# The lo parts of phase 1 on VectorE: weight splits and turned parts leave GpSimd, which keeps the rotation of q and k

## The chip, the cores and the metric

The kernel runs on one core of one Trainium2 chip. The metric is device time in microseconds of one launch, the median of several runs. The program is written in a tile framework that puts the instructions of each engine into a fixed order when the kernel is built, by a timeline that it plays through itself; on the chip every engine works through its own queue in that order and waits on semaphores of the others.

## What is computed

One layer of a decoder over a prompt of 2048 tokens (width 1024) and 8 decode tokens. What matters here is its front part:

```python
h = rmsnorm(x, g_mix) * (1 + sc_m) + sh_m
proj = h @ w_in                                   # 1024 -> 2560
conv_in, q, k, v = split(proj)                    # 1024, 512, 512, 512 columns
u = conv_in[..., :512] * sigmoid(conv_in[..., 512:])
conv_out = silu(layernorm(causal_dwconv(u_ext, dw_w, dw_b)))   # width 31
q, k = partial_rope(q), partial_rope(k)           # first 16 of each 64 columns are rotated
```

Attention with two softmax maps per head, the output projection and a SwiGLU network follow; the change does not touch their code. All of it is float32.

## The kernel before

**Numbers in two parts.** The matrix products are made from operands split in two: `hi` is the float32 value rounded to the matmul type (a copy on ScalarE, ACT), and `lo = raw - hi` is a subtraction. A product is three matmuls (`mm3`, lines 152 to 156): hi by lo, lo by hi, hi by hi. `split_sb` (lines 187 to 189) does both steps for an operand that lies in SBUF; its last argument names the engine of the subtraction, and without one it is GpSimd (POOL).

**Phase 1** (`phase1`, from line 288) makes the projections. It is a row of ten units: k, conv 0, v, conv 1, q for the first 1024 tokens, then conv 0, k, conv 1, v, q for the second (lines 556 to 584). A unit takes 512 columns of `w_in`. `weights` (line 400) loads them as eight raw tiles of 128x512, one for each block of 128 input channels, and splits each (line 414): `wh` on ACT, `wl` on POOL for blocks 0, 2, 4 and 6 (`POOLW`, line 43) and on VectorE (DVE) for the other four. There are 9 buffers for `wh` (line 42), so that one block of the next unit can be split ahead of time and the others when the unit before them lets its own go. `wl` and the raw tiles share 12 slots, and the `wl` of a block is written into the slot of the raw tile one block before it (line 398), so each split waits for the one before.

A **conv unit** (line 450) makes two groups of 128 channels, each as two blocks of 512 tokens: 24 matmuls for the gate, 24 for the value. The product with the sigmoid goes into `u` (line 470, DVE), and the depthwise convolution is a chain of one instruction of 1024 columns on DVE at line 474 and 30 at line 477, each adding one tap to `y`. These chains, 8 of them with 240 instructions at line 477, are most of the work of DVE.

A **nat unit** (line 519; k, v or q) makes eight tiles of 128 tokens by 512 columns: 24 matmuls into `one` (two buffers), then `ev` on ACT (line 531, two buffers), for q and k the rotation in place on POOL (`rope`, lines 498 to 501, four small instructions), a store, and in `emit` (line 503) the split of the turned tile into `parts` (two buffers): hi on ACT, lo on POOL for every v tile and for the even tiles of q and k, on DVE for their odd tiles (lines 511 and 516). `parts` is stored (lines 512, 517) and read back by attention. All loads and stores are issued from one queue (SP), at lines 123 and 126.

Between the tiles of the units, `turn` (line 357) prepares the next 512 tokens: transposes on the tensor engine (PE), `hx` on ACT, `hTh` on ACT and `hTl` on DVE. `ada_steps` (line 428) puts matmuls of 9 rows between the others.

Of the kernel before, what the change touches and what calls it, by code (L numbers as in the profile page):

```python
# [27 lines left out]
HD = 64  # L28
# [11 lines left out]
CONV_LATE = 0  # L40
XB, YB, SGB = 4, 2, 1
WHB, WSL, ASL = 9, 12, 3
POOLW = (0, 2, 4, 6)

# [36 lines left out]
class Kern:  # L83
# [204 lines left out]
    def phase1(self, ctx):  # L288
        nc, tc, I, O = self.nc, self.tc, self.I, self.O
# [8 lines left out]
        if True:  # L298
# [101 lines left out]
            def weights(src, c0, c1=None):  # L400

                out = []
                for k in range(KD):
# [9 lines left out]
                    wh = self.t(wp, [P, 512], F32R, "wh", bufs=WHB)  # L413
                    self.split_sb(wh, wl, raw, nc.gpsimd if k in POOLW else nc.vector)
                    out.append((wh, wl))
# [87 lines left out]
            def emit(kind, dst, tt):  # L503
                rows = slice(tt * P, (tt + 1) * P)
                b, own = tt // 4, slice((tt % 4) * P, (tt % 4 + 1) * P)
                if kind != "q":
                    self.st(O[kind + "_prompt"][0, 0].rearrange("t h d -> t (h d)")[rows], dst)
                pt = self.t(wp, [P, 2 * NH * P], F32R, "parts", bufs=2)
                if kind == "v":
                    v = pt.rearrange("p (i n) -> p i n", i=2)  # L510
                    self.split_sb(v[:, 0], v[:, 1], dst)
                    self.st(self.vD[b][own].rearrange("t i n -> t (i n)"), pt.bitcast(F32))
                else:

                    v = pt.rearrange("p (g r d) -> p g r d", r=2, d=HD)
                    self.split_sb(v[:, :, 0], v[:, :, 1], dst.rearrange("p (g d) -> p g d", d=HD), nc.vector if tt % 2 else None)
                    self.st((self.kD if kind == "k" else self.qD)[b][own].rearrange("t h r d -> t (h r d)"), pt.bitcast(F32))

            def nat_unit(kind, half, then=()):
                w = weights(I["w_in"], {"q": 1024, "k": 1536, "v": 2048}[kind])  # L520
                for i in range(8):
                    if i in then:
                        then[i]()
                    tt = 8 * half + i
                    hh, hl = hT[tt // 4]
                    po = self.ps1()
                    ts_ = slice((tt % 4) * P, (tt % 4 + 1) * P)
                    for k in range(KD):
                        self.mm3(po, hh[:, k, ts_], hl[:, k, ts_], w[k][0], w[k][1], k == 0, k == KD - 1)
                    ev = self.t(wp, [P, 512], F32, "ev", bufs=2)  # L530
                    nc.scalar.activation(ev, po, AF.Copy, scale=QSCALE if kind == "q" else 1.0)  # L531
                    if kind != "v":
                        rope(ev, tab[:, tt, :], P)
                    emit(kind, ev, tt)
                if half == 0:
                    pd = dec_proj(w)
                    ev = self.t(wp, [P, 512], F32, "ev", bufs=2)[:DEC]
                    nc.scalar.activation(ev, pd[:DEC], AF.Copy, scale=QSCALE if kind == "q" else 1.0)
                    if kind != "v":
                        rope(ev, tabd, DEC)  # L540
                    self.st({"q": self.qsD, "k": self.ksD, "v": self.vsD}[kind], ev)
                    if kind != "q":
                        self.st(O[kind + "_sample"].rearrange("o b s h d -> (o b s) (h d)"), ev)
# [994 lines left out]
```

## Time and profile before

| | us |
|---|---|
| median of 3 runs | 2752.56 (2746.84 to 2755.15) |
| the profiled execution | 2752.62 |
| its span, first to last instruction | 2750.4 |

Mean granted TensorE clock 0.974. Busy shares of the span: PE 94%, its weight loads 79%, DVE 70%, ACT 46%, POOL 52%.

A line of the profile names the line of the kernel, the engine, the operation and the tiles that it writes and reads. Idle time of an engine is put down to what released it. Two things need care: matmuls are pipelined, so that a duration of 0.39 us stands beside a start-to-start distance of 0.23 us; and an instruction that waits inside its engine, having been started, counts as busy.

### The profile page before, as it was taken

The page shows a single profiled execution, that of the slowest core. Times are in us where ns is not written, and L with a number is a line of the kernel's source. Part 1 is how long each engine was busy: PE and PEld are TensorE (multiplying, and loading weights), DVE is VectorE, ACT ScalarE, POOL GpSimd, SP SyncE. Part 2 cuts the span into 40 slices and gives each one's busy share as a digit, 9 for nine tenths or more (in the row PEclk, how much of TensorE's full clock was granted, in tenths as well). Part 3 has the DMA queues.
Part 4 walks back from the last instruction along what each step waited for, and adds up shares of the span by engine and source line. Part 5 has one row for each costly group of instructions (what it writes and reads, how often), then busy time and mean ns, then how long its engine had stood idle before and what let it go on. Part 6 is the DMA issues. An engine that isn't in the chain of part 4 may idle for free.

```text
span 2750.4 us, 38187 instructions
## 1 busy us (share of the span) xinstructions
PE 2572.3 (94%) x13470; PEld 2162.1 (79%) x13470; DVE 1921.5 (70%) x2833; ACT 1252.6 (46%) x2385; POOL 1422.3 (52%) x974
## 2 busy tenths in 40 slices
PE   8998999997899997999799999999999999999997
PEld 3475767676688766787799999999899997777875
DVE  2267889995988878767677777676866652455467
ACT  4433231225798766373436343553444334333333
POOL 2125355444732223233576877677877753464573
PEclk9999999998999998999899999999999999999998
DMA  8634232336732223252334333434334435766555
GB/s 277 203 110 175 66 131 100 119 137 185 233 97 89 85 81 124 99 166 100 107 123 144 113 125 113 154 113 127 110 121 131 131 113 195 249 204 223 161 175 181
DMA packets 343993, 391.25 MB, mean 142 GB/s; under 512 B 31829, under 2 KB 258272, under 8 KB 343794
## 3 DMA queue, kind: packets, MB, share of 16 engines
q1 hardware_dynamic: 335945, 370.80, 41.7%
q10 hardware_dynamic: 7856, 18.01, 1.9%
q8 instruction: 106, 1.74, 0.3%
q14 instruction: 86, 0.70, 0.1%
HBM read 283.10 MB, written 106.12 MB: 142 GB/s over the span
## 4 chain that ended last, share of the span: by engine, by line
PE 54%; DVE 9%; issue 7%; POOL 7%; DMA 3%; ACT 2%; SPq 1%; ACTq 0%; POOLq 0%; DVEq 0%
PE in L1161 26%; PE o L1341 10%; PE one L155 2%; PE one L156 2%; PE one L154 2%; DVE p L660 2%; POOL wl L189 1%; PE two L655 1%; PE two L656 1%; PE x L844 1%; PE x L154 1%; POOL w L1273 1%; POOL z L1273 1%; PE x L156 1%; PE x L155 1%
## 5 line engine op out<-in xcount | busy, mean ns | idle before, releaser
L1341 PE MATMUL o<-b,a 128*128 128x512 f32 x1848 | 433.3, 396 | 14.1 <-POOL b L189 11.8
L1341 PEld LDWEIGHTS o<-b,a 128*128 128x128 f32 x1848 | 348.9, 189 | 97.9 <-POOL b L189 12.5
L1161 PE MATMUL in<-cls,wh 128*128 128x344 f32 x1056 | 336.0, 325 | 30.4 <-DVE nat L1164 13.4
L189 POOL TENSOR_TENSOR wl<-wr,wh 128x512 fp32r<-128x512 f32 x198 | 294.2, 1494 | 112.9 <-ACT wh L188 111.8
L1161 PE MATMUL in<-chs,wl 128*128 128x344 f32 x1056 | 341.9, 324 | 7.8 <-DVE wl L189 7.8
L477 DVE SCALAR_TENSOR_TENSOR y<-u,cw,y 128x1024 f32<-128x1024 f32 x240 | 338.5, 1439 | 2.7
L1161 PE MATMUL in<-chs,wh 128*128 128x344 f32 x1056 | 339.9, 322 | 0.0
L1161 PE MATMUL in<-cla,wh 128*128 128x344 f32 x792 | 256.6, 324 | 1.2 <-ACT wh L188 0.7
L188 ACT CAST wh<-tr 128x512 fp32r<-128x512 f32 x264 | 162.3, 618 | 205.0 <-PE in L1161 179.7
L1161 PE MATMUL in<-cha,wl 128*128 128x344 f32 x792 | 254.9, 322 | 0.0
L1161 PE MATMUL in<-cha,wh 128*128 128x344 f32 x792 | 252.4, 321 | 0.0
L189 POOL TENSOR_TENSOR wl<-tr,wh 128x512 fp32r<-128x512 f32 x132 | 203.8, 1548 | 83.4 <-ACT wh L188 79.6
L672 POOL TENSOR_TENSOR p<-p,p 128x384 f32<-128x384 f32 (+9 forms) x60 | 109.1, 1819 | 260.3 <-ACT p L671 210.5
L1161 PEld LDWEIGHTS in<-cls,wh 128*128 128x128 f32 x1056 | 199.4, 190 | 34.0 <-DVE nat L1164 14.0
L1161 PEld LDWEIGHTS in<-chs,wl 128*128 128x128 f32 x1056 | 200.9, 190 | 8.9 <-DVE wl L189 8.9
L189 POOL TENSOR_TENSOR b<-wr,b 128x512 fp32r<-128x512 f32 x77 | 126.0, 1650 | 156.4 <-ACT b L188 155.1
L189 POOL TENSOR_TENSOR w<-w,wh 128x512 fp32r<-128x512 f32 x40 | 86.0, 2150 | 231.6 <-ACT wh L188 113.0
L1161 PEld LDWEIGHTS in<-chs,wh 128*128 128x128 f32 x1056 | 201.4, 191 | 0.0
L189 DVE TENSOR_TENSOR a<-gr,a 128x1032 fp32r<-128x1032 f32 (+1 forms) x77 | 116.4, 1518 | 109.7 <-ACT a L188 109.5
L154 PE MATMUL one<-w,hTh 128*128 128x512 f32 x384 | 156.6, 411 | 16.1 <-ACT ev L531 10.3
L188 ACT CAST wh<-wr 128x512 fp32r<-128x512 f32 x198 | 122.4, 620 | 104.0 <-POOL wl L189 43.9
L664 ACT ACTIVATE p<-p,st 128x384 f32<-128x384 f32 (+15 forms) x128 | 156.1, 1221 | 25.1 <-DVE st L660 20.1
(353 smaller groups left out, 6554.9 us busy)
## 6 DMA issues: line engine op xcount, KB each, us to landing
wr<-in_w_ffn_in SPq DMA_DIRECT2D x132, 512.0 KB
gD<-xt SPq DMA_DIRECT2D x64, 516.0 KB
wr<-in_w_ffn_out SPq DMA_DIRECT2D x99, 256.0 KB
gr<-gD SPq DMA_DIRECT2D x44, 516.0 KB
w<-in_w_in SPq DMA_DIRECT2D x80, 256.0 KB
gr<-gD SPq DMA_DIRECT2D x33, 512.0 KB
xt<-in_x_prompt SPq DMA_DIRECT2D x32, 512.0 KB
a<-in_w_ada SPq DMA_DIRECT2D x64, 256.0 KB
```

The lines of the kernel that those rows point to most:

```text
L154: mm(ps, lhsT=wh, rhs=xl, start=start, stop=False)
L155: mm(ps, lhsT=wl, rhs=xh, start=False, stop=False)
L156: mm(ps, lhsT=wh, rhs=xh, start=False, stop=stop)
L188: self.nc.scalar.copy(out=hi, in_=raw)
L189: (eng or self.nc.gpsimd).tensor_tensor(out=lo, in0=raw, in1=hi.bitcast(F32), op=ALU.subtract)
L477: nc.vector.scalar_tensor_tensor(out=y, in0=u[:, j:j + HALF], scalar=self.cw[:, ct, j:j + 1], in1=y, op0=ALU.mult, op1=ALU.add)
L660: dv.tensor_tensor_reduce(out=pc[:, lo:hi], in0=sc[:, 0:w], in1=add, scale=1.0, scalar=m, op0=ALU.add, op1=ALU.min, accum_out=mo)
L664: nc.scalar.activation(pc[:, 0:L], pc[:, 0:L], AF.Exp, bias=m, scale=-1.0, accum_out=l)
L672: nc.gpsimd.tensor_tensor(out=a, in0=a, in1=b, op=ALU.add)
L1161: nc.tensor.matmul(ps, lhsT=wt[:, k, :], rhs=xt[:, k, :], start=not more and k == 0 and j == 0, stop=k == 3 and j == 2, skip_group_check=True)
L1273: op = lambda e, o, x, y, k: e.tensor_tensor(out=o, in0=x, in1=y, op=k)
L1341: mm = lambda x, y, s, e: nc.tensor.matmul(ps[i], lhsT=a[:, x, sl], rhs=b[:, y], start=s, stop=e, skip_group_check=True)
```

## The change

`POOLW` becomes empty, so that all eight `wl` of a unit are made on DVE, and the `parts` of all tiles of v, q and k get their lo on DVE. The rotation (lines 498 to 501) stays on POOL. That is 10 units by 4, or 40, weight splits and 16 v tiles and 16 even tiles of q and k, or 32, splits of `parts`: 72 instructions of 128x512 change engine. ACT, PE and the transfers get the same instructions as before.

```diff
-POOLW = (0, 2, 4, 6)
+POOLW = ()
...
                 if kind == "v":
                     v = pt.rearrange("p (i n) -> p i n", i=2)
-                    self.split_sb(v[:, 0], v[:, 1], dst)
+                    self.split_sb(v[:, 0], v[:, 1], dst, nc.vector)
...
                     v = pt.rearrange("p (g r d) -> p g r d", r=2, d=HD)
-                    self.split_sb(v[:, :, 0], v[:, :, 1], dst.rearrange("p (g d) -> p g d", d=HD), nc.vector if tt % 2 else None)
+                    self.split_sb(v[:, :, 0], v[:, :, 1], dst.rearrange("p (g d) -> p g d", d=HD), nc.vector)
```

## Rows read from the trace of the kernel before

**Rows 1.** The page: span, and busy time of each engine.

```profile
span 2750.4 us, 38187 instructions
PE 2572.3 (94%) x13470; PEld 2162.1 (79%) x13470; DVE 1921.5 (70%) x2833; ACT 1252.6 (46%) x2385; POOL 1422.3 (52%) x974
```

**Rows 2.** Busy time by stretch: length, PE, PEld, DVE, ACT, POOL, granted clock, DMA.

```profile
138.00:414.00 276.00, 257.08 (x1051) 181.56 (x1050) 213.83 (x201) 82.47 (x128) 122.70 (x76) 0.97 0.35 120
414.00:620.00 206.00, 193.40 (x791) 146.49 (x790) 192.52 (x161) 45.19 (x77) 99.59 (x72) 0.98 0.33 119
```

**Rows 3.** What PE waited for, 138 to 620 us: total, times, longest.

```profile
PE one L154 <- ACT ev L531: 9.3, 1, 9.3
PE two L155 <- POOL w L189: 8.7, 7, 2.1
PE one L154 <- DVE w L189: 4.4, 2, 4.0
PE two L155 <- DVE w L189: 3.1, 6, 1.4
```

**Rows 4.** Groups by line, 138 to 650 us: busy, mean ns, idle before.

```profile
L477 DVE SCALAR_TENSOR_TENSOR y<-u,cw,y 128x1024 f32<-128x1024 f32 x240 | 338.5, 1439 | 2.7
L500 POOL TENSOR_TENSOR rope<-ev,tab 128x64 f32<-128x64 f32 x25 | 22.8, 913 | 0.0
```

**Rows 5.** Line 189, 138 to 650 us: ns min/median/max, first and last start.

```profile
L189 DVE TENSOR_TENSOR w<-w,wh x36: 677/680/1775, 137.3 to 603.9; 128x512 fp32r<-128x512 f32 x36
L189 POOL TENSOR_TENSOR w<-w,wh x35: 1263/2128/13826, 139.0 to 600.3; 128x512 fp32r<-128x512 f32 x35
L189 POOL TENSOR_TENSOR parts<-ev,parts x28: 1262/1504/22977, 205.7 to 641.6; 128x512 fp32r<-128x512 f32 x28
L189 DVE TENSOR_TENSOR parts<-ev,parts x13: 677/693/1750, 142.4 to 647.6; 128x512 fp32r<-128x512 f32 x13
```

**Rows 6.** Timeline, 560 to 563 us, POOL and DVE: start, duration.

```profile
560.03 1.29 POOL L189 TENSOR_TENSOR parts<-ev,parts 128x512 fp32r<-128x512 f32 x1 [2.19 <-ACT parts L188]
...
560.04 2.36 DVE L477 SCALAR_TENSOR_TENSOR y<-u,cw,y 128x1024 f32<-128x1024 f32 x1
...
562.33 1.27 DVE L477 SCALAR_TENSOR_TENSOR y<-u,cw,y 128x1024 f32<-128x1024 f32 x1
```

**Rows 7.** Timeline, 203 to 233 us, POOL, DVE and ACT.

```profile
205.73 24.20 POOL L189 TENSOR_TENSOR parts<-ev,parts 128x512 fp32r<-128x512 f32 x2 [4.01 <-ACT parts L188]
...
217.94 9.64 DVE L477 SCALAR_TENSOR_TENSOR y<-u,cw,y 128x1024 f32<-128x1024 f32 x8
...
228.74 0.60 ACT L531 ACTIVATE ev<-one 128x512 f32<-128x512 f32 x1 [14.46 <-POOL parts L189]
```

**Rows 8.** Timeline, 260 to 278 us, start of a conv unit, DVE.

```profile
267.58 0.69 DVE L189 TENSOR_TENSOR w<-w,wh 128x512 fp32r<-128x512 f32 x1
268.19 1.28 DVE L477 SCALAR_TENSOR_TENSOR y<-u,cw,y 128x1024 f32<-128x1024 f32 x1
...
271.80 0.68 DVE L189 TENSOR_TENSOR w<-w,wh 128x512 fp32r<-128x512 f32 x1
```

**Rows 9.** Timeline, 580 to 592 us, start of the last q unit, DVE and ACT.

```profile
579.79 10.69 DVE L477 SCALAR_TENSOR_TENSOR y<-u,cw,y 128x1024 f32<-128x1024 f32 x8
590.40 0.68 DVE L189 TENSOR_TENSOR w<-w,wh 128x512 fp32r<-128x512 f32 x1
...
582.64 0.62 ACT L188 CAST wh<-w 128x512 fp32r<-128x512 f32 x1
```

**Rows 10.** Busy time by stretch, as rows 2, around two of the waits.

```profile
230.00:240.00 10.00, 10.00 (x39) 8.00 (x38) 2.49 (x3) 5.46 (x8) 2.94 (x3) 0.81 0.83 299
...
590.00:600.00 10.00, 7.53 (x20) 5.75 (x21) 9.96 (x8) 2.29 (x3) 6.61 (x3) 0.66 0.26 92
```

**Rows 11.** What DVE and SP's queue waited for, 138 to 620 us: total, times, longest.

```profile
DVE parts L189 <- ACT parts L188: 14.7, 6, 6.1
...
SPq L126 <- POOL parts L189: 87.7, 22, 23.3
```

## The prediction

> **What bounds the kernel now.** I read the page first. TensorE (PE) is busy for 94% of the span and no other engine for more than 70% [rows 1], so time can be won only where PE stands idle, and lost only where it is made to. The change touches phase 1 alone, so the second view is busy time by stretch over the part of phase 1 in which the convolution runs. PE is idle for 276 - 257.1 = 18.9 us from 138 to 414 and for 206 - 193.4 = 12.6 us from 414 to 620, together 31.5 us. DVE has 62 us free in the first stretch and only 13.5 us in the second, where it is busy for 93% [rows 2]. The third view, what PE waited for there, names 25.5 us of the 31.5 in four rows: 9.3 us in one piece for an `ev` of a nat unit, and 8.7 + 4.4 + 3.1 = 16.2 us for weight splits, on POOL and on DVE [rows 3].
>
> The view of line 189 shows why these are late. The same subtraction takes 0.68 us on DVE, and on POOL 1.26 us at best, 2.13 us as a median for weights, and 23.0 us at worst [rows 5]. The timeline shows a mechanism behind it: a convolution instruction of 1.27 us takes 2.36 us when a POOL split starts beside it, so the two don't run together, one waits for the other [rows 6]. Over all 240 the mean is 1.439 us, which is 240 x (1.439 - 1.27) = 41 us of waiting inside DVE [rows 4, 6]. The opposite case costs more: from 205.7 us a split of `parts` sat on POOL for 23.0 us while DVE went through its chain without a break (eight instructions in 9.64 us at the end of it); only then could `ev` be refilled, after ACT had stood for 14.46 us behind POOL, and PE lost its 9.3 us [rows 3, 5, 7].
>
> **The change, part by part.** The profiled execution took 2752.62 us, 2.2 us more than its span, and stands on the median of the runs (2752.56). The sum is made against it.
>
> *The `parts` on DVE.* The 9.3 us go if `ev` no longer depends on a POOL split. A v tile has no rotation, so after the change its way is ACT, ACT, DVE, with 0.69 us on DVE [rows 5]. I take the whole 9.3 us. What could be late next is the same split in DVE's own queue, behind convolution instructions of 1.2 us each; with two buffers of `ev` and some 5 us of matmuls to a tile, one or two of them are covered. Stores of `parts` also leave SP's queue sooner: SP stood for 87.7 us, once for 23.3 us, behind POOL splits, with the loads of weights queued behind [rows 11]. That I cost at nothing, since none of the rows of PE names those loads.
>
> *The weight splits on DVE.* At the start of a conv unit two DVE splits stand 271.80 - 267.58 = 4.22 us apart with one POOL split between, 2.11 us for a block [rows 8]. With both on DVE and one convolution instruction after each, a block takes 0.61 + 1.2 = 1.8 us [rows 7, 8]; with none 0.6 us; with two 3.0 us. PE needs about 1.8 us: 48 matmuls of 512 columns at 0.23 us over 8 blocks are 1.4, and the decode and adaLN matmuls come between (an estimate). So at the middle value the waits nearly vanish, at 3.0 they grow. I take the middle, since DVE's queue now shows splits and chain in turn, and leave a third: 11 of the 16.2 us are won, with 16.2 as the upper end and a loss as the other (it is a rival below).
>
> *What DVE pays.* In the stretch to 650 us, 35 + 28 = 63 splits move [rows 5], at 0.61 us from start to start that is 38 us. Against it stands the 41 us of waiting, of which the rotation keeps a part: its instructions are more (25 tiles of four in this stretch) but their mean is 0.913 us with waiting included [rows 4], against 1.26 us alone for a split. I give the splits 26 of the 41, bounds 0 and 41. DVE thus has between 3 us less and 38 us more to do, 12 at my value, spread over both stretches. The 75.7 us of idle time cover it in sum; if that cover is gone it is gone in the second stretch.
>
> *A wait that is added.* DVE takes its queue in order. A lo of a turned tile waits for hi, which waits for the rotation, and the convolution stands behind. Today that is 14.7 us in six waits for 13 such instructions [rows 5, 11]; 12 even tiles of q and k join them here (28 less 16 of v), so at the same rate 12 x 14.7 / 13 = 13.6 us of DVE. The lower end is 0, since the rotation no longer queues behind splits on POOL. PE feels it where DVE has no room, the second stretch: I take 4 us.
>
> *The clock.* After the two longest waits the granted clock shows the lower level, 1.2 of 2.4 GHz, for part of a slice: 0.81 in the 10 us after the first, which is 1.9 us of matmul time lost, and 0.66 around the second, 3.4 us less the 2.5 in which PE was idle anyway [rows 10]. Between 2.8 and 5.3 us come back with the waits, I take 4.
>
> The Trainium skill ("SBUF — State Buffer", Who interferes with whom) calls the port that VectorE and GpSimd share an exclusive lock: whoever issues first holds it for one instruction and the other blocks. By that alone a POOL split would wait for one DVE instruction, the 9.3 us would not be this mechanism's, and the forecast would be 11 us of gain, about 2742. The 2.36 us agree with it and the 23.0 us do not, so the measurement decides.
>
> **Sum.** -9.3 - 11 - 4 + 4 = -20.3 us: 2752.6 - 20.3 = 2732. PE is the bound before and after phase 1, so an earlier end of it is passed on.
>
> **Rivals.**
> *DVE's order starves the splits (slower).* The fixed order may put two convolution instructions, not one, between two weight splits: 3.0 us for a block against 2.11 today. Over the seven blocks that are not split ahead this is 7 x 0.9 = 6.2 us for each start where PE already waits; for four starts (three conv units and the last q unit) 25 us, less the 9.3 won: 2752.6 + 15.7 = 2768. It decides from the point where the mean distance passes 2.11 us. For it: in the last q unit `wh` was done at 583.3 us and its DVE split came at 590.4, with eight convolution instructions before it [rows 9]. Against it: those were themselves late through POOL's splits. Chance 0.18.
>
> *DVE becomes the bound (no change).* In the second stretch DVE has 13.5 us free [rows 2]; 13.6 us of new waits and a relief smaller than I took would fill them. PE's waits then change their name and the 9.3 us are eaten later: 2746 to 2755. Chance 0.18. The Trainium skill ("Perfetto Trace Analysis", Optimizing Scalar/DVE Operations) has a rule for this side: with DVE saturated, work may be better off on another engine, which the change undoes; it adds that the shared port may take the benefit away. In the second stretch the trace has DVE at 93%, so both halves bear on it.
>
> *The rotation is starved instead (a smaller gain).* Two of 63 splits met DVE's chain without a break, 23.0 and 13.8 us [rows 5]. The rotation stays on POOL and DVE's queue gets denser. One such case costs the 9.3 us and its clock again: 2743. Chance 0.08.
>
> *All waits go (more).* 9.3 + 16.2 + 5.3 = 31 us with no added wait, and four even tiles of the last q unit, 1.5 us each, off the chain into attention: 2752.6 - 37 = 2716. Chance 0.10. The change doing something else than it says is no rival: the diff names the engine in each of the three calls.
>
> **How the numbers follow.** The forecast has 0.46. About 0.3% (8 us) can be told from no change here. Faster by more: forecast, the larger gain and most of the starved case, 0.63. The no-change case and the rest of the starved one, 0.19. Slower 0.18. The range runs from 2713, the larger gain with some room for a changed order elsewhere, to 2765, most of the way to the slower case.
>
> **What would show it.** Right: no POOL split and no piece of 9 us before line 154; DVE weight splits under 2 us apart at conv starts; line 477 at a mean near 1.33 us; clock 1.00 after 230 us. Wrong: waits of PE for `w` on DVE above 16 us in sum, waits of DVE for ACT `parts` above 25 us, or a POOL rotation instruction of 10 us.

## The result, and the profile after

| | before | after |
|---|---|---|
| median (range), us | 2749.70 (2743.52 to 2755.15) | 2719.46 (2719.03 to 2723.68) |
| ratio, 95% interval | | 0.9887 (0.9872 to 0.9903) |
| span of the profiled execution, us | 2750.4 | 2717.6 |
| mean granted clock | 0.974 | 0.978 |

The change makes the kernel 30 us faster, 1.1%. The forecast was 20 us; the time lies inside the range and nearest to the rival "all waits go" (2716).

Busy time by stretch after the change, columns as in rows 2:

```profile
138.00:414.00 276.00, 273.37 (x1124) 190.90 (x1123) 225.40 (x243) 81.98 (x129) 40.90 (x42) 0.99 0.37 125
414.00:620.00 206.00, 195.51 (x815) 152.64 (x813) 180.42 (x187) 51.80 (x89) 54.25 (x63) 0.98 0.39 137
```

Against [rows 2], PE's idle time from 138 to 414 us falls from 18.9 to 2.6 us; from 414 to 620 it is 10.5 after 12.6. The measure that I use below is the end of phase 1, read as the last start of a matmul at line 154 into `one` (first and last start stand behind the durations in ns; the count in the last field is of a sample). First before, then after:

```profile
L154 PE MATMUL one<-w,hTh x384: 387/395/797, 47.0 to 643.7; 128*128 128x512 f32 x192
```

```profile
L154 PE MATMUL one<-w,hTh x384: 387/395/628, 47.3 to 618.3; 128*128 128x512 f32 x192
```

Phase 1 ends 25.4 us earlier, and the other 5 to 7 us come later. What PE waited for after the change, 138 to 620 us:

```profile
PE two L155 <- DVE w L189: 5.4, 5, 2.1
PE one L154 <- DVE w L189: 4.8, 6, 1.6
PE one L154 <- ACT ev L531: 1.8, 1, 1.8
PE two L367 <- ACT hx L368: 0.5, 1, 0.5
```

Three smaller rows of the same view before, beside those of [rows 3]:

```profile
PE two L367 <- ACT hx L368: 3.1, 2, 2.1
PE one L154 <- POOL w L189: 1.3, 1, 1.3
PE two L154 <- ACT wh L188: 1.2, 1, 1.2
```

The one wait of 9.3 us of [rows 3] is gone, 1.8 us of its kind are left, and 10.2 us for weight splits remain where there were 16.2 (17.5 with the row of 1.3). Two other profiles of the same sequence of instructions, both among the runs below, have 9.9 and 13.3 us here, so 3 us more or less in this sum tell nothing. The chain at line 477, 138 to 650 us, as in [rows 4], and line 189 as in [rows 5]:

```profile
L477 DVE SCALAR_TENSOR_TENSOR y<-u,cw,y 128x1024 f32<-128x1024 f32 x240 | 307.8, 1305 | 2.1
```

```profile
L189 DVE TENSOR_TENSOR w<-w,wh x70: 671/685/945, 137.8 to 582.1; 128x512 fp32r<-128x512 f32 x70
L189 DVE TENSOR_TENSOR parts<-ev,parts x41: 676/691/947, 140.5 to 622.3; 128x512 fp32r<-128x512 f32 x41
```

The chain's mean falls from 1.439 to 1.305 us, which is 240 x 0.134 = 32 us of waiting inside DVE, against 38 us of splits that came onto it. No split takes longer than 0.95 us; on POOL two had taken 13.8 and 23.0.

The start of the second conv unit shows what became of [rows 8]. Timeline of DVE after the change:

```profile
248.30 0.69 DVE L189 TENSOR_TENSOR w<-w,wh 128x512 fp32r<-128x512 f32 x1 [1.84 <-ACT wh L188]
248.91 1.28 DVE L477 SCALAR_TENSOR_TENSOR y<-u,cw,y 128x1024 f32<-128x1024 f32 x1
...
255.35 0.69 DVE L189 TENSOR_TENSOR w<-w,wh 128x512 fp32r<-128x512 f32 x1
255.96 1.28 DVE L477 SCALAR_TENSOR_TENSOR y<-u,cw,y 128x1024 f32<-128x1024 f32 x1
...
257.22 0.69 DVE L189 TENSOR_TENSOR w<-w,wh 128x512 fp32r<-128x512 f32 x1
```

and of the same place before, ACT and DVE:

```profile
255.06 1.13 ACT L188 CAST wh<-w 128x512 fp32r<-128x512 f32 x2
...
262.49 0.69 DVE L189 TENSOR_TENSOR w<-w,wh 128x512 fp32r<-128x512 f32 x1
```

Before, the first split came 6.3 us after two `wh` were ready (255.06 + 1.13), because the instructions ahead of it in DVE's queue were late; after, DVE stood waiting for `wh` and the split began at once. The trace before shows a way from the held split of v [rows 7] to this late start. SP issued nothing from 205.4 us until the store of that split at 228.73; the loads of the next x tiles went out at 237.51 us, where they go out at 224.67 after the change; and DVE stood 5.58 us for sums that ACT makes from these tiles. SP and DVE before, then SP after:

```profile
228.73 0.35 SPq L126 DMA_DIRECT2D vD<-parts  x1
...
237.51 2.89 SPq L123 DMA_DIRECT2D xt<-in_x_prompt  x4
...
250.14 0.17 DVE L139 TENSOR_SCALAR rsq<-ss 128x4 f32<-128x4 f32 x1 [5.58 <-ACT sq L347]
```

```profile
224.67 1.76 SPq L123 DMA_DIRECT2D xt<-in_x_prompt  x4
```

From 255.35 on, three splits follow at 1.87 us, split and convolution instruction in turn, which is the distance that I had worked out. Over the whole start it is not kept. The table has the four starts that the prediction counted, read from the starts of the splits at line 189 and the ends of the casts to `wh` at line 188: how long after the first `wh` the first split began, and the mean distance of the seven splits.

| start of | conv 1, first half | conv 0, second half | conv 1, second half | last q |
|---|---|---|---|---|
| first split late, before, us | 6.8 | 3.7 | 1.1 | 8.2 |
| first split late, after, us | 0.0 | 1.6 | 2.6 | 0.0 |
| distance per block, before, us | 2.25 | 2.35 | 2.48 | 2.24 |
| distance per block, after, us | 2.11 | 2.46 | 2.56 | 3.60 |

So the change did not make the splits follow faster; it made them begin earlier. The two starts that were late by 7 and 8 us are those behind a v unit.

### The profile page after: what moved, and what is told of

It is laid out like the page before. It is cut to its first block, busy times and chain, and to the rows that moved or that the text cites. A ratio compares the mean times of both kernels' runs of the same rounds, so it can differ in the third digit from the quotient of the medians.

```text
span 2717.6 us, 38141 instructions
## 1 busy us (share of the span) xinstructions
PE 2563.3 (94%) x13470; PEld 2154.6 (79%) x13470; DVE 1913.7 (70%) x2905; ACT 1250.5 (46%) x2385; POOL 1268.9 (47%) x902
## 4 chain that ended last, share of the span: by engine, by line
PE 51%; DVE 10%; issue 8%; POOL 5%; DMA 2%; ACT 2%; SPq 0%; ACTq 0%; POOLq 0%; DVEq 0%
PE in L1161 26%; PE o L1341 8%; PE one L155 2%; PE one L156 2%; PE one L154 2%; DVE p L660 2%; POOL wl L189 1%; PE two L655 1%; PE two L656 1%; PE x L844 1%; POOL w L1273 1%; POOL z L1273 1%; PE x L154 1%; DVE p L675 1%; PE x L156 1%
## 5 line engine op out<-in xcount | busy, mean ns | idle before, releaser
L1341 PEld LDWEIGHTS o<-b,a 128*128 128x128 f32 x1848 | 348.0, 188 | 97.1 <-POOL b L189 12.2
L477 DVE SCALAR_TENSOR_TENSOR y<-u,cw,y 128x1024 f32<-128x1024 f32 x240 | 307.8, 1305 | 2.1
L498 POOL TENSOR_TENSOR ropet<-ev,tab 128x128 f32<-128x128 f32 x32 | 21.4, 670 | 433.5 <-ACT ev L531 433.1
L1161 PEld LDWEIGHTS in<-cls,wh 128*128 128x128 f32 x1056 | 199.0, 190 | 30.8 <-DVE nat L1164 10.8
```

What stands on the lines that cost most here:

```text
L477: nc.vector.scalar_tensor_tensor(out=y, in0=u[:, j:j + HALF], scalar=self.cw[:, ct, j:j + 1], in1=y, op0=ALU.mult, op1=ALU.add)
L1161: nc.tensor.matmul(ps, lhsT=wt[:, k, :], rhs=xt[:, k, :], start=not more and k == 0 and j == 0, stop=k == 3 and j == 2, skip_group_check=True)
L1341: mm = lambda x, y, s, e: nc.tensor.matmul(ps[i], lhsT=a[:, x, sl], rhs=b[:, y], start=s, stop=e, skip_group_check=True)
```

## The experiments

Two theories stood against each other. **Port:** a two-input subtraction on POOL and one on DVE exclude each other, so that what the change wins is time of DVE and of held-back POOL splits. **Chain length:** a split on POOL is simply longer than one on DVE (2.1 against 0.7 us), and what waits behind it waits longer. A second question was how the gain divides between weights and turned parts. Ratios are to the kernel before on the same chip (medians 2750.8 us for the first four, 2751.6 for the next four, 2753.3 for the last four); "end" is the end of phase 1 as read above, in each run's own profile.

An edit also makes the framework set a new order: in the traces PE's instructions follow each other differently before and after the change, so most runs vary the engine and the order together. Two do not, as is said there. A profile is of one execution, which need not be near the median: that of the spare work took 2765.9 us, those of the parts alone 2718.3 and 2734.1. The end of phase 1 is steadier: three profiles of the change's sequence of instructions have 618.3, 617.2 and 616.6 us.

| run | median, us | ratio, 95% interval | end, us |
|---|---|---|---|
| weights only | 2739.29 | 0.9962 (0.9950 to 0.9975) | 631.3 |
| parts only | 2723.23 | 0.9907 (0.9891 to 0.9923) | 611.5 |
| v parts only | 2733.92 | 0.9940 (0.9922 to 0.9957) | 618.9 |
| spare work on POOL | 2760.19 | 1.0031 (1.0019 to 1.0042) | 653.5 |
| rotation on DVE too | 2719.35 | 0.9892 (0.9872 to 0.9912) | 612.0 |
| weights first | 2722.02 | 0.9898 (0.9877 to 0.9919) | 616.6 |
| even q and k parts only | 2742.31 | 0.9971 (0.9957 to 0.9986) | 631.5 |
| all weights on POOL | 2739.23 | 0.9953 (0.9934 to 0.9972) | 628.6 |
| the change again | 2722.84 | 0.9888 (0.9871 to 0.9904) | 617.2 |
| parts only again | 2731.03 | 0.9913 (0.9900 to 0.9927) | 610.3 |
| two blocks on POOL | 2728.25 | 0.9911 (0.9897 to 0.9925) | 617.9 |
| rotation on DVE, weights shared | 2717.59 | 0.9867 (0.9851 to 0.9884) | 603.8 |

### Weights only

```diff
-POOLW = (0, 2, 4, 6)
+POOLW = ()
```

> The 40 weight splits on DVE, the lo of the turned parts as before (v and even tiles on POOL). Both theories (the shared port; the length of the chain from raw weight to split weight) expect PE's waits for w to fall from 16.2 us to about 10, as in the full change. The wait of 9.3 us for ev hangs on a POOL split of v that was held back, and stays in the port theory if DVE's chain runs without a break there again. Time 2749.7 - 6 to -10 and 2 of clock: 2737 to 2742; 2728 if the held-back split does not come again. Mean at line 477 between 1.36 and 1.40 us.

11.5 us, inside the expected range, but not for the reason given. What PE waited for, 138 to 620 us:

```profile
PE one L154 <- DVE w L189: 8.1, 9, 2.3
PE two L155 <- DVE w L189: 7.4, 9, 1.5
```

15.5 us of waiting for weights, with all of them on DVE, where there were 16.2 [rows 3]. What went is the wait for `ev`, which fell to 0.7 us: in this order of work the longest hold of a split of v was 7.5 us, not 23. The starts behind the two v units stayed late, by 6.6 and 6.5 us. ACT and DVE at the second conv unit:

```profile
245.25 1.13 ACT L188 CAST wh<-w 128x512 fp32r<-128x512 f32 x2
...
252.42 0.69 DVE L189 TENSOR_TENSOR w<-w,wh 128x512 fp32r<-128x512 f32 x1
```

DVE had no wait of 5.58 us there, so that wait is not the only way to a late start. Chain length alone did not make PE wait less for weights.

### Parts only

```diff
-POOLW = ()
+POOLW = (0, 2, 4, 6)
```

(against the changed kernel, so that only `emit` differs from the kernel before)

> The lo of all turned parts on DVE, the weight splits shared with POOL as before. The 9.3 us for ev and the clock after it go, PE's waits for w stay near 16 us: 2749.7 - 9.3 - 2 = 2738. If the weights were the whole gain, 2750. Mean at line 477 about 1.37 us.

27.6 us, nearly the whole effect and 15 us more than expected. With the weights shared between POOL and DVE as before, PE waited for them far less, 138 to 620 us:

```profile
PE two L155 <- DVE w L189: 2.6, 3, 1.4
PE two L155 <- POOL w L189: 2.5, 3, 1.5
...
PE one L154 <- POOL w L189: 0.7, 1, 0.7
```

5.8 us against 17.5 before (all four kinds of row) and 10.2 after the full change. The starts behind the v units are in time, 0.1 and 0.7 us after the first `wh`. ACT and DVE at the second conv unit:

```profile
246.03 1.13 ACT L188 CAST wh<-w 128x512 fp32r<-128x512 f32 x2
...
246.73 0.69 DVE L189 TENSOR_TENSOR w<-w,wh 128x512 fp32r<-128x512 f32 x1 [0.22 <-issue]
```

The engine of the weight splits was thus not what made them late; the turned parts on POOL were. A rival is that the raw weights came earlier, since their loads share SP's queue with the stores of `parts`. ACT's waits for these loads, before and here, 138 to 620 us, speak against it:

```profile
ACT wh L188 <- DMA w<-in_w_in: 22.6, 24, 3.3
```

```profile
ACT wh L188 <- DMA w<-in_w_in: 21.6, 23, 1.9
```

### The v parts only, and the even q and k parts only

(both against the kernel before)

```diff
-                    self.split_sb(v[:, 0], v[:, 1], dst)
+                    self.split_sb(v[:, 0], v[:, 1], dst, nc.vector)
```

> Only the 16 v tiles on DVE; q and k as before. If the gain of the parts is the one held-back v split, this gives all of it: 2738 to 2740, the same as with all parts within 3 us. If the even tiles of q and k count (rotation no longer behind a split on POOL), 3 to 8 us above the run with all parts.

```diff
-..., nc.vector if tt % 2 else None)
+..., nc.vector)
```

> Only the 16 even tiles of q and k go to DVE; v and the weights as before. Parts add up: all parts gave 27.6 us, v alone 16.9, so 10.7 here, 2740. If the gain of v is the same one as that of q and k (DVE ahead of its backlog), 2735 or less.

16.9 and 9.2 us (by their intervals 12 to 21 and 4 to 12), together 26.1 of the 27.6: in time they add up as far as these intervals tell (in the end of phase 1, 24.8 and 12.2 against 32.2, they overlap a little), and v is the larger half, though both move 16 instructions. The second run keeps v on POOL, and the hold comes back almost to the nanosecond. POOL and ACT in its timeline:

```profile
204.83 24.20 POOL L189 TENSOR_TENSOR parts<-ev,parts 128x512 fp32r<-128x512 f32 x2 [4.01 <-ACT parts L188]
...
227.84 0.60 ACT L531 ACTIVATE ev<-one 128x512 f32<-128x512 f32 x1 [14.46 <-POOL parts L189]
```

Both lines have the durations of [rows 7], a microsecond earlier. The longest of PE's waits in that run:

```profile
PE one L154 <- ACT ev L531: 9.3, 1, 9.3
```

So the piece of 9.3 us belongs to v on POOL, as the prediction had it, and it is no accident of one execution; it also needs an order of work near that of the kernel before, since with the weights moved it did not come. Its removal alone leaves 7.6 us of v's gain. I put them down to the starts behind the v units: 0.1 and 0.8 us late with the v parts on DVE, 7.6 and 9.4 in the run that keeps them on POOL. In all profiles these two starts are late by more than 6 us where v is split on POOL (the kernel before, weights only, even q and k only), and by less than 1 us in every run that splits v on DVE, whatever the rest of the edit.

### Spare work on POOL

```diff
+            spare = wp.tile([P, 512], BF16, tag="spare", name="spare")
...
                     out.append((wh, wl))
+                    nc.gpsimd.tensor_tensor(out=spare, in0=wh.bitcast(F32), in1=wh.bitcast(F32), op=ALU.subtract)
```

(added to the changed kernel)

> The full change, and behind each of the 80 weight splits one more POOL subtraction of 128x512 that reads wh twice and writes a spare tile that nobody reads. Port theory: the chain at line 477 is held up again, mean from 1.305 back to 1.40 to 1.47 us, DVE has 25 to 40 us more to do, PE waits longer for w on DVE, time 2719 + 8 to 25 us. Chain-length theory: nothing waits for these instructions, time 2719 within 5 us.

The time goes up to 2760.2 us, some 40 us above the changed kernel and 9 us above the kernel before, although nothing reads what these 80 instructions write. The order is not the reason: in the traces POOL has the changed kernel's sequence with the spare instructions put in, and of the first 900 instructions of DVE four have moved, by at most three places. That rules out chain length as the whole story and goes beyond what the port theory had asked for. The line of the spare instructions, the chain at line 477 and PE's waits:

```profile
L415 POOL TENSOR_TENSOR spare<-wh x71: 1030/1482/2022, 142.8 to 603.6; 128x512 bf16<-128x512 f32 x71
```

```profile
L477 DVE SCALAR_TENSOR_TENSOR y<-u,cw,y 128x1024 f32<-128x1024 f32 x240 | 327.5, 1386 | 2.1
```

```profile
PE one L154 <- DVE w L189: 17.3, 14, 3.2
PE two L155 <- DVE w L189: 12.3, 5, 3.2
```

The chain's mean rises to 1.386 us only, 19 us in sum and a little under what was expected; but the spare work comes in bursts at the starts of units, just where DVE splits weights, and there it counts for more. Timeline of DVE and POOL at such a start:

```profile
491.36 1.52 DVE L189 TENSOR_TENSOR w<-w,wh 128x512 fp32r<-128x512 f32 x1
492.80 1.52 DVE L189 TENSOR_TENSOR parts<-ev,parts 128x512 fp32r<-128x512 f32 x1
494.25 3.45 DVE L477 SCALAR_TENSOR_TENSOR y<-u,cw,y 128x1024 f32<-128x1024 f32 x2
497.62 0.80 DVE L189 TENSOR_TENSOR w<-w,wh 128x512 fp32r<-128x512 f32 x1
```

```profile
490.32 4.91 POOL L415 TENSOR_TENSOR spare<-wh 128x512 bf16<-128x512 f32 x3
```

Splits of 0.69 us take 1.52, between the two splits of weights shown lie 6.3 us, where the same two stand 3.3 us apart in the changed kernel (without the split of `parts` between them, 0.6 us there), and PE waits 29.6 us for weights on DVE instead of 10.2. At the four starts of the table above a block takes 3.07, 3.47, 3.69 and 4.05 us, about 1 us more at three of them and 0.45 at the last, while the first splits are as late as in the changed kernel. One thing is mixed in: the rotation queues behind the spare instructions on POOL. ACT's waits for the rotation's last instruction rose from 80 to 90 us, and PE's for `ev` from ACT are 1.2 us, so this carries little of the 40.

### Rotation on DVE too

```diff
-                gp = nc.gpsimd
+                gp = nc.vector
```

(in `rope`, against the changed kernel)

> The full change and the rotation of q and k on DVE too, so that POOL does nothing beside the convolution. Port theory: line 477 comes down to 1.27 to 1.28 us (6 to 8 us less for DVE), but 128 small instructions of some 0.2 to 0.3 us (32 us) come onto DVE, and they wait in its queue for ev on ACT. If free port time decides, 2712 to 2719; if DVE's room from 414 us on decides, 2722 to 2735. I lean to the second.

2719.35 us, the same as the change, at the upper end of the first case; I had leaned to the second. With POOL empty the chain runs at the length of a single instruction:

```profile
L477 DVE SCALAR_TENSOR_TENSOR y<-u,cw,y 128x1024 f32<-128x1024 f32 x240 | 302.1, 1279 | 1.9
```

6 us less for the chain pay for part of the rotation's instructions, which take 0.2 to 0.3 us each on DVE. DVE's room was not the limit.

### Weights first

```diff
+                    with tc.high_priority():
-                    self.split_sb(wh, wl, raw, nc.gpsimd if k in POOLW else nc.vector)
+                        self.split_sb(wh, wl, raw, nc.gpsimd if k in POOLW else nc.vector)
```

> The full change with the weight splits set ahead of other work when the order is made. If PE's remaining 10.2 us for w on DVE come from the place of the splits behind convolution instructions in DVE's queue, they fall to under 5 us and the time to 2710 to 2715; if they come from late raw weights, 2719 within 4 us. A split that stands early in DVE's queue and waits for its weight holds the convolution: then above 2723.

2722.0 us, no difference from the change that can be told. The edit asked for another order and got none: in the traces PE, DVE, ACT and POOL have the same sequence of instructions as in the changed kernel. So the run is one more measurement of the change and tests none of the three cases. It gives the spread of the waits for weights (7.0 and 6.3 us here).

### All weights on POOL

```diff
-POOLW = ()
+POOLW = (0, 1, 2, 3, 4, 5, 6, 7)
```

> All turned parts on DVE, all 80 weight splits on POOL, twice as many as before. Chain-length theory: a block takes 2.1 us or more in a row on POOL where PE needs 1.8, PE waits for w on POOL above 20 us in sum, 2740 to 2755. Theory that only the turned parts mattered and weights are covered by early starts: 2723 within 6 us.

2739.2 us, just under the range of the chain-length theory, but PE's waits for w on POOL are 12.7 us in sum, not above 20. The chain has the highest mean of all runs, 1.446 us, above the kernel before.

### The change, and the parts alone, again; two blocks on POOL; rotation on DVE with weights shared

> The full change once more, on the same chip as the next three: 31 us under the kernel before, ratio 0.988 to 0.990.

> All turned parts on DVE, weights shared with POOL as before. If the weight splits are worth nothing once the parts are off POOL, within 4 us of the full change; if they keep the 11.5 us that they had alone, 11 us above it.

The change is 30.4 us under the kernel before, as at first. The parts alone are 8.2 us above it on the same chip, in the first pair of ratios 5 us (0.9907 against 0.9887): between the two cases expected. Yet their phase 1 ends 7 us earlier than that of the change, and did so in both profiles: 611.5 and 610.3 against 618.3 and 617.2. The parts alone give it back in attention, and not always as much. Line 655, the scores of attention, of the two profiles of that one program (last start behind the word "to"):

```profile
L655 PE MATMUL two<-KS,QB x320: 220/397/796, 617.9 to 1024.5; 128*128 128x512 f32 x136, 128*128 128x128 f32 x8, 128*128 128x256 f32 x8, 128*128 128x384 f32 x8
```

```profile
L655 PE MATMUL two<-KS,QB x320: 218/397/795, 616.8 to 1034.7; 128*128 128x512 f32 x136, 128*128 128x128 f32 x8, 128*128 128x256 f32 x8, 128*128 128x384 f32 x8
```

The same instructions begin a microsecond earlier and end ten later. The first of these executions was the fastest of its five and the second the slowest of its six. Attention adds a spread of that size to any gain of phase 1, and what sets it was not tried; so it stays open why the change, whose phase 1 ends later, is the faster of the two.

```diff
-POOLW = ()
+POOLW = (0, 4)
```

> All turned parts on DVE, weight blocks 0 and 4 on POOL, six on DVE. If DVE's room and the port balance each other between none and four blocks on POOL, the optimum is flat: within 4 us of the full change. A gain of more than 4 us would say that DVE's own splits are the next wait.

2728.3 us, 5 us above the change, a little beyond the 4 us that I had allowed; the two intervals overlap, so the optimum is flat as far as this shows.

```diff
-POOLW = ()
+POOLW = (0, 2, 4, 6)
...
-                gp = nc.gpsimd
+                gp = nc.vector
```

> All turned parts and the rotation on DVE, the four even weight blocks on POOL, so that POOL does weights alone. DVE gets 32 us of rotation and loses 24 us of weights, the port is taken by 40 long splits: mean at line 477 about 1.36 us, time 2719 to 2732; under 2715 would mean that the rotation on POOL is what the port still costs.

2717.6 us (2715.7 to 2719.2), a little below the expected range, and the earliest end of phase 1 of all, 40 us before that of the kernel before:

```profile
L154 PE MATMUL one<-w,hTh x384: 387/395/505, 47.8 to 603.8; 128*128 128x512 f32 x192
```

It is the lowest median of all, 5 us under the change on the same chip. The two intervals overlap, so I call it no worse, and better in phase 1. The chain's mean was 1.340 us, so the port was not free there: which work shares it mattered, not only how much. A POOL split was held there for longer than in any other run, and a second one for 24.85 us:

```profile
194.64 31.06 POOL L189 TENSOR_TENSOR w<-w,wh 128x512 fp32r<-128x512 f32 x1 [4.24 <-ACT hx L368]
```

It is the block that is split ahead of its unit, whose other splits begin at 240.9 us, and PE has no wait beside it: a hold costs what waits behind it.

## Why the prediction was right, and where its sum was off

**The v split that was held back: right, and priced too low.** Of the 9.3 us of waiting 7.5 went, v alone is worth 16.9 us of time, and the run that kept v on POOL brought them back. The stores behind such a split were costed at nothing, "since none of the rows of PE names those loads". The loads of x stood in that queue as well, and through ACT and DVE they reach the late start of the second conv unit.

**The weight splits: the step that failed.** "A block takes 0.61 + 1.2 = 1.8 us" held for part of one start (1.87); over the four starts a block takes 2.11 to 3.60 us, where it took 2.24 to 2.48. Nor did "11 of the 16.2 us are won": 6 were won, and moving the weights alone won 0.7 of the wait. I had read the waits for `w` as the price of splits on POOL. Those that went were the price of starts that were late by 7 and 8 us behind the v units, and what removed that was the v parts leaving POOL. In phase 1 the weights' half of the change is worth 12.4 us alone (643.7 to 631.3) and costs 7 us once the parts are gone (611.5 to 618.3). The two halves remove the same backlog, so their gains don't add, while those of v and of the even q and k tiles nearly do.

**What DVE pays: right in kind, small in size.** I gave the splits 26 of 41 us of relief; 32 came. Against 38 us of new work that leaves 6, not 12.

**The wait that is added: right.** DVE's waits for ACT `parts`, 138 to 620 us, rose from 14.7 us [rows 11] by 12.2, where 13.6 was forecast:

```profile
DVE parts L189 <- ACT parts L188: 26.9, 19, 6.5
```

That it cost PE 4 us is not seen: from 414 to 620 us DVE is busy for 180.42 us, where it was 192.52, and PE's idle time fell. The prediction contradicts itself here: it named waits above 25 us as a sign of being wrong and forecast 14.7 + 13.6 = 28.3. That sign came, and "splits under 2 us apart at conv starts" did not; the other signs came out as for a right forecast.

**The clock: right where it was read.** From 138 to 414 us the granted clock is 0.99 after 0.97 [rows 2], and the slice from 230 to 240 us is at 1.00 after 0.81 [rows 10]. From 414 to 620 us it stays at 0.98, so the second half of this term did not come; from 565 to 575 us, around the waits that the last q unit still has, it is 0.83.

**Passed on.** Phase 1 gave 25.4 us, and the sum of 20.3 was meant for it. By the rows of PE the terms came out at 7.5 for `ev` (9.3 forecast), 6 for the weights (11), nothing for the added wait (-4), and about 5 for the clock (4; an estimate, 276 us at 0.99 in place of 0.97). The three smaller rows, which the prediction left out, give 5 more. So the terms for `ev` and the weights were 7 us too large, the small rows and the added wait made up 9, and that the sum lies this near is partly luck. The rest came in attention, which the prediction had taken as unchanged.

**Rivals.** "DVE's order starves the splits" came in its condition and not in its price. The mean distance at the four starts does not fall below the 2.11 us that were to decide, and in the last q unit splits stand 3.1 to 3.3 us apart with two convolution instructions between; PE's 4.8 us of waits at line 154 mostly fall there. But that start begins at once, where it was 8.2 us late, so PE did not lose by it in sum. Timeline of DVE after the change:

```profile
560.45 0.69 DVE L189 TENSOR_TENSOR w<-w,wh 128x512 fp32r<-128x512 f32 x1 [0.17 <-ACT wh L188]
...
573.88 0.68 DVE L189 TENSOR_TENSOR w<-w,wh 128x512 fp32r<-128x512 f32 x1
...
577.13 0.69 DVE L189 TENSOR_TENSOR w<-w,wh 128x512 fp32r<-128x512 f32 x1
...
580.19 0.69 DVE L189 TENSOR_TENSOR w<-w,wh 128x512 fp32r<-128x512 f32 x1
```

"DVE becomes the bound" fell: the run that put the rotation on DVE as well lost nothing. "The rotation is starved" fell too, its longest instruction took 1.88 us:

```profile
L498 POOL TENSOR_TENSOR ropet<-ev,tab x32: 443/469/1882, 64.2 to 620.0; 128x128 f32<-128x128 f32 x32
```

"All waits go" had the time nearly right with the wrong path: 10.2 us of waits for weights are still there.

**What stays open.** How much of the gain is the engine and how much the new order was not separated. Shown are the port's price, by the spare work in an unchanged order, and the late starts, which go with v on POOL in every order that was run.

## What to carry to other kernels

An elementwise instruction on GpSimd beside a busy VectorE need not be free help: look first whether VectorE's own instructions get longer at the same moments, and count that as its cost. Leave it there where nothing waits behind it: the run with the lowest median keeps 40 weight splits on GpSimd. When an engine works through a fixed order, a wait for one product is often the backlog left by another, so before pricing a wait by the length of the instruction it names, see when that instruction could have started. Try the halves of such a change alone, since the gains from removing one backlog don't add.

## What was not expected of the hardware

A POOL subtraction was passed over for 23.0 us by DVE instructions that followed each other without a gap, and this came again as 22.98 us in the run with even q and k parts only. It was no rare case: with weights shared, splits on POOL were held for 10.8 us (parts only) up to 31.1 us (rotation on DVE, weights shared). In the kernel before, the split ended 1.1 us after the last of the eight convolution instructions of [rows 7], when DVE had nothing to do. At other moments POOL got in after one instruction [rows 6]; what decides between the two was not found. The Trainium skill ("SBUF — State Buffer", Who interferes with whom) says of the shared port that whoever issues first has it for the whole instruction and the other fully blocks. The 1.52 us splits beside the spare work agree with it; that the blocked side gets in after that one instruction, as the prediction read it, is what the 23 us speak against.

The second is the price of work that nobody waits for: 80 subtractions on POOL, 1.03 us each at best, made the kernel some 40 us slower, half a microsecond each, by delaying DVE at the moments when PE depended on it.
